# Moving the block sums of the second MLP product into the first, and reordering buffers and the last pair, in an encoder-layer kernel

## The chip, the cores and the metric

The kernel runs on one core of a Trainium2 chip. The metric is the device time of one launch in microseconds (us). The kernel before takes 2404.65 us, the median of three runs (2403.71 to 2405.92).

## The reference

One encoder layer works on two sequences of width 1024: 2048 rows (prompt) and 256 rows (sample), 18 row tiles of 128 in all. Cut to the part that matters here:

```python
def encoder_layer(x, c, ...):
    ...                                   # modulation, mixer: everything before the MLP
    h = modulate(rmsnorm(x, norm_mlp), sh2, sc2)
    x = x + gt2[:, None, :] * (jnp.square(jax.nn.relu(h @ w_mlp_in)) @ w_mlp_out)
    return x
def run_trunk(x, c, ...):
    ...
    return rmsnorm(x, norm_final)
```

`w_mlp_in` is 1024 x 4096 and `w_mlp_out` 4096 x 1024, all in float32.

## The kernel before

Everything up to the mixer's output fills the first 970 us and is untouched. Then come two matrix products, each done as a 2 x 2 block product in seven multiplications instead of eight (`STEPS`, L27: left operand, right operand, accumulator bank X, Y or Z). Four of the seven left operands are sums: S1 to S4, formed from the blocks A11, A12 and A22 and from A21. Each float32 operand is split into a high part (ScalarE cast, L80, `split`) and a low part (VectorE subtraction, L81), and each multiplication is run three times (`three`): high by high, low by high, high by low.

**First product** (L1023 to L1071), about 971 to 1671 us. Three column groups `c` of three row pairs each (a pair is two row tiles), and in each group eight blocks `q` of 512 hidden columns, in the order 0 to 7. The stationary operand is the weight (`wB`, `wT`), the moving one the activation (`opA`, `opS`, 128x384). At the start of groups 1 and 2 VectorE and ScalarE also form the left operands of the group (`form_left`). Each `q` gives two hidden tiles `hid` (ReLU and square on ScalarE, L1055 to L1059), each stored to DRAM in `hidd[c][r]`, where `r = q // 2` is the round of the second product that will read it. For round 3 alone (`j // GJ == NG - 1`, L1062 and L1068) VectorE also forms S2, S3 and S4 in a tile `hs` and S1 in `hid`, and stores seven blocks instead of four (`NB`, L979).

**Second product** (L1152 to L1205). Four rounds `r` over the hidden dimension and, in each, nine pairs `pr`. `load_mo` (L1099) loads the round's weights into raw tiles `t` and `o` (five buffers "raw", two "rawb"), forms sums and splits them into 28 tiles `wo`; there are just 28, so that a weight tile of the next round needs the same tile of the last pair to be done. A pair loads its left blocks into `hr` (pool `hr0` for even `pr`, `hr1` for odd, L1162), forms the four sums on VectorE where only four blocks were stored (L1166 to L1170), splits seven operands into `ho`, multiplies, and adds the banks into `acc` (L1194 on ScalarE in round 0, else L1196 on VectorE). `acc` comes from DRAM and goes back there between rounds. With nine pairs the last pair of a round and the first of the next both use `hr0`. In round 3 `finish_tile` (L1128) multiplies by the gate, adds the residual, normalises and stores; the last pair has its own version, `finish_block` and `finish_rows` (L1138, L1143).

The order of each engine's instructions is set by a scheduler at build time, which also decides where pools let a tile start. Pools lie at addresses in the order in which they are opened (`VB`, L1078), and a pool's tile waits for whatever was at its address before.

Of the kernel before, what the change touches and what calls it, by code (L numbers as in the profile page):

```python
# [31 lines left out]
def encoder(ctx: ExitStack, tc: tile.TileContext, a):  # L32
# [43 lines left out]
    def dram(shape, name):  # L76
        return tc.dram_tile(shape, F32, name=nm(name))
# [901 lines left out]
    NB = [4] * (NG - 1) + [7]  # L979
    hidd = [[dram([NPC, GJ, P, NB[r] * P], "hidd") for r in range(NG)] for _ in range(NC)]  # L980

    def raw_w(s):
        return wt("raw", s, [P, 1024], 8)
# [37 lines left out]
    for c in range(NC):  # L1021
        if c:
            left = left_ops()  # L1023
            for pr in range(NPC):
                hab = []
                for i in range(2):
                    h = raw_w("hr")
                    sp.dma_start(out=h, in_=h2d[2 * (NPC * c + pr) + i])
                    hab.append(h)
                form_left(left, pr, *hab, lambda s: wt("s", s, [P, 512], 4))  # L1030
        for q in range(8):
            w = load_mi(q)
            hid = [wt("hid", "hid", [P, NPC, 4, P], 3) for _ in range(2)]
            at, cp_ = [{}, {}], [{}, {}]
            for i, (ln, rn, bn) in enumerate(STEPS):
                for f in range(2):
                    if i in (0, 1, 3):
                        at[f][bn] = bank(bn)
                    o, kept = at[f][bn], cp_[f]
                    lh, ll = left[ln]  # L1040
                    rh, rl = w[rn]
                    three(lambda p_, k, first, last: add_mm(
                        i, o[:, :CW], (rh, rh, rl)[p_][:, k * 256 + f * P:k * 256 + f * P + P],
                        (lh, ll, lh)[p_][:, k], first, last), range(4))
                    if i in (0, 2, 3):
                        kept[i] = mid("c")
                        act.copy(kept[i], o[:, :CW])
                    hf = hid[f]
                    if i == 1:
                        dve.tensor_tensor(out=hf[:, :, 0, :], in0=cols(o), in1=cols(kept[0]), op=ALU.add)  # L1050
                    elif i == 4:
                        dve.tensor_tensor(out=hf[:, :, 2, :], in0=cols(o), in1=cols(kept[3]), op=ALU.add)
                    elif i == 5:
                        dve.tensor_tensor(out=hf[:, :, 1, :], in0=cols(o), in1=cols(kept[2]), op=ALU.add)
                        act.activation(hf[:, :, 0:3, :], hf[:, :, 0:3, :], AF.Relu)  # L1055
                    elif i == 6:
# [11 lines left out]
                        if j // GJ == NG - 1:  # L1068
# [66 lines left out]
    def halves(b):  # L1135
        return slice(b % 2 * 512, b % 2 * 512 + 512)

    def finish_block(b, y, x1, ss):  # L1138
        dve.tensor_tensor(out=y, in0=y, in1=gate[:, halves(b)], op=ALU.mult)
        dve.tensor_tensor(out=y, in0=y, in1=x1[:, halves(b)], op=ALU.add)  # L1140
        act.activation(x1[:, halves(b)], y, AF.Square, accum_out=ss[:, b % 2:b % 2 + 1])  # L1141

    def finish_rows(t, y, ss):  # L1143
        dve.tensor_tensor(out=ss[:, 2:3], in0=ss[:, 0:1], in1=ss[:, 1:2], op=ALU.add)
        r = rstd_from(ss[:, 2:3], 1, 1.0 / D)
        for b in range(2):
            yb = y[:, 512 * b:512 * b + 512]
            dve.scalar_tensor_tensor(out=yb, in0=yb, scalar=r[:, 0:1], in1=nf[:, halves(b)],
                                     op0=ALU.mult, op1=ALU.mult)
            sp.dma_start(out=xrows("y", t)[:, halves(b)], in_=yb)  # L1150

    for r in range(NG):  # L1152
        w = load_mo(r)
        if r == NG - 1:
            gate = load_gate(1, 0, lambda s: v1(s, "rawb"))
            nf = v1("nf", "rawb")
            sp.dma_start(out=nf, in_=a["norm_final"].rearrange("(o c) -> o c", o=1).to_broadcast([P, D]))
        for pr in range(NT // 2):
            if r == NG - 1 and pr == NP // 2:
                gate = load_gate(1, 1, lambda s: v1(s, "rawb"))  # L1160
            c, pc = divmod(pr, NPC)
            hv = v1("hr", f"hr{pr % 2}").rearrange("p (j b s) -> p j b s", j=GJ, b=7)  # L1162
            sp.dma_start(out=hv[:, :, 0:NB[r], :].rearrange("p j b s -> p j (b s)"),
                         in_=hidd[c][r][pc].rearrange("j p n -> p j n"))
# [6 lines left out]
            acc = v1("acc", "acc").rearrange("p (b n) -> p b n", b=4)  # L1171
            if r:
                sp.dma_start(out=acc, in_=accd[pr].rearrange("p (b n) -> p b n", b=4))
            rows = [acc[:, 2 * i:2 * i + 2, :].rearrange("p b n -> p (b n)") for i in range(2)]
            end = r == NG - 1 and pr == NT // 2 - 1
            if r == NG - 1:
                x1 = [v1("x1", "raw") for _ in range(2)]
                for i in range(2):
                    sp.dma_start(out=x1[i], in_=x1d[2 * pr + i])
            at = {}  # L1180
            ss = [tsm([P, 4], "ss") for _ in range(2)] if end else None
            for i, (ln, rn, bn) in enumerate(STEPS):
# [14 lines left out]
                if end:  # L1197
                    if i not in (0, 2, 3):
                        finish_block(b_, acc[:, b_], x1[b_ // 2], ss[b_ // 2])
                    if i > 4:  # L1200
                        finish_rows(2 * pr + b_ // 2, rows[b_ // 2], ss[b_ // 2])
                elif r == NG - 1 and i > 4:
# [78 lines left out]
```

## Time and profile before

| | |
|---|---|
| profiled execution | 2405.53 us, of which the span is 2403.5 us |
| median of the runs | 2404.65 us |
| TensorE busy | 2326.6 us, 97% of the span |
| VectorE busy | 1539.2 us, 64% |
| ScalarE busy | 1004.5 us, 42% |
| first product | about 971 to 1671 us |
| second product | 1671 us to the end |

A row of the timeline gives start, duration, engine, line, operation, output and input tiles, shapes and count, and in brackets the idle time before it with what ended it. PE is TensorE's multiplication, PEld its weight load, DVE VectorE, ACT ScalarE, POOL GpSimd, SPq the queue that issues transfers. Busy rows overlap a little at their ends, since an instruction's tail runs beside the next one's start.

### The profile page before, as it was taken

How to read it: one execution, taken by the hardware profiler on the slowest of the kernel's cores; microseconds unless marked ns; L12 is line 12 of the kernel's file. 1: busy time of each engine (PE TensorE's matmuls, PEld its weight loads, DVE VectorE, ACT ScalarE, POOL GpSimd, SP SyncE). 2: the span in 40 equal slices, each digit the busy share in tenths (PEclk: the TensorE clock that was granted, in tenths of full speed). 3: DMA queues.
4: the chain of work that ended last, by engine and by line, in shares of the span. 5: the costliest groups of instructions: out<-in, count | busy, mean ns of one | idle time of the engine just before them, and what ended most of it. 6: DMA issues, size and time to landing. Idle time of an engine off the chain costs nothing.

```text
span 2403.5 us, 30791 instructions
## 1 busy us (share of the span) xinstructions
PE 2326.6 (97%) x11905; PEld 2033.9 (85%) x11905; DVE 1539.2 (64%) x2254; ACT 1004.5 (42%) x1686; POOL 115.8 (5%) x191
## 2 busy tenths in 40 slices
PE   7999999999999999999999999999899999999998
PEld 4788887788887888999999999998787788787786
DVE  3676768535444754655785577557756867857788
ACT  4842222223333533555665566556334323224332
POOL 0101100011111000000000000000000000000000
PEclk9999999999999999999999999999999999999999
DMA  8647568433333455543453346433534545546774
GB/s 286 215 144 252 188 217 289 171 99 121 119 103 127 140 171 188 167 131 123 154 184 123 127 156 194 136 120 130 191 105 159 200 158 197 188 158 227 276 255 165
DMA packets 183866, 411.69 MB, mean 171 GB/s; under 512 B 12101, under 2 KB 80485, under 8 KB 176809
## 3 DMA queue, kind: packets, MB, share of 16 engines
q1 hardware_dynamic: 182136, 405.68, 49.2%
q0 software_dynamic: 1584, 4.06, 0.6%
q8 instruction: 93, 1.52, 0.3%
q14 instruction: 53, 0.43, 0.1%
HBM read 274.15 MB, written 135.54 MB: 170 GB/s over the span
## 4 chain that ended last, share of the span: by engine, by line
PE 77%; issue 9%; DVE 6%; DMA 5%; ACT 2%; POOL 1%; SPq 0%; POOLq 0%; DVEq 0%; ACTq 0%
PE mX L963 30%; PE proj L84 18%; PE mZ L963 15%; PE mY L963 7%; PE o L84 2%; DMA ada<-ada_w 1%; PE dft L84 1%; PE tr L745 1%; DMA hr<-hidd 1%; DVE woT L81 1%; PE kvf L84 1%; DVE adacc L356 1%; DVE woB L81 1%; PE sc L84 1%; DVE acc L1196 1%
## 5 line engine op out<-in xcount | busy, mean ns | idle before, releaser
L963 PE MATMUL mX<-woT,ho 128*128 128x512 f32 x1296 | 311.5, 390 | 3.7 <-ACT x L1141 1.5
L80 ACT CAST ho<-hr 128x512 fp32r<-128x512 f32 x252 | 153.1, 621 | 343.3 <-PE mX L963 208.7
L963 PEld LDWEIGHTS mX<-woT,ho 128*128 128x128 f32 x1296 | 242.8, 188 | 56.3 <-issue 1.9
L963 PE MATMUL mX<-opS,wT 128*128 128x384 f32 x1152 | 208.0, 334 | 0.0
L84 PE MATMUL proj<-whi,hhi 128*128 128x512 f32 x720 | 190.1, 402 | 18.3 <-ACT hhi L80 9.4
L963 PEld LDWEIGHTS mX<-opS,wT 128*128 128x128 f32 x1152 | 200.4, 188 | 0.0
L81 DVE TENSOR_TENSOR ho<-hr,ho 128x512 fp32r<-128x512 f32 x252 | 170.4, 687 | 39.7 <-ACT ho L80 39.5
L84 PE MATMUL proj<-wlo,hhi 128*128 128x512 f32 x720 | 185.2, 396 | 0.0
L84 PE MATMUL proj<-whi,hlo 128*128 128x512 f32 x720 | 184.4, 393 | 0.0
L84 PEld LDWEIGHTS proj<-whi,hhi 128*128 128x128 f32 x720 | 132.4, 190 | 47.4 <-ACT hhi L80 10.7
L84 PEld LDWEIGHTS proj<-wlo,hhi 128*128 128x128 f32 x720 | 136.1, 191 | 30.7 <-issue 2.5
L84 PEld LDWEIGHTS proj<-whi,hlo 128*128 128x128 f32 x720 | 133.1, 188 | 30.7 <-issue 4.2
L81 DVE TENSOR_TENSOR wB<-mr,wB 128x1024 fp32r<-128x1024 f32 x72 | 88.0, 1222 | 81.1 <-ACT wB L80 81.0
L1196 DVE TENSOR_TENSOR acc<-mX,acc 128x512 f32<-128x512 f32 x117 | 80.0, 687 | 68.5 <-PE mX L963 55.5
L963 PE MATMUL mY<-woB,ho 128*128 128x512 f32 x432 | 112.2, 396 | 10.0 <-ACT woB L80 6.8
L963 PE MATMUL mX<-woB,ho 128*128 128x512 f32 x432 | 110.8, 396 | 5.6 <-ACT ho L80 5.5
L963 PE MATMUL mZ<-woT,ho 128*128 128x512 f32 x432 | 108.9, 392 | 6.3 <-ACT woT L80 5.5
L105 POOL TENSOR_SCALAR rv<-ss 128x1 f32<-128x1 f32 (+1 forms) x72 | 17.9, 248 | 1885.8 <-ACT x L139 1391.9
L80 ACT CAST wB<-mr 128x1024 fp32r<-128x1024 f32 x72 | 75.4, 1047 | 76.0 <-PE mY L963 41.0
L963 PEld LDWEIGHTS mY<-woB,ho 128*128 128x128 f32 x432 | 81.7, 190 | 30.1 <-ACT woB L80 8.3
L963 PE MATMUL mY<-opA,wB 128*128 128x384 f32 x576 | 104.6, 334 | 2.3 <-DVE x L153 2.3
L963 PE MATMUL mX<-opA,wB 128*128 128x384 f32 x576 | 105.5, 334 | 0.0
(251 smaller groups left out, 4368.9 us busy)
## 6 DMA issues: line engine op xcount, KB each, us to landing
mr<-w_mlp_in SPq DMA_DIRECT2D x96, 512.0 KB
hidd<-hid SPq DMA_DIRECT2D x48, 768.0 KB
hr<-hidd SPq DMA_DIRECT2D x27, 1024.0 KB
accd<-acc SPq DMA_DIRECT2D x27, 1024.0 KB
acc<-accd SPq DMA_DIRECT2D x27, 1024.0 KB
ada<-ada_w SPq DMA_DIRECT2D x48, 512.0 KB
h<-hd SPq DMA_DIRECT2D x36, 512.0 KB
x<-x_prompt SPq DMA_DIRECT2D x32, 512.0 KB
```

The costliest lines, as they stand in the source:

```text
L80: act.copy(hi, src)
L81: dve.tensor_tensor(out=lo, in0=src, in1=hi.bitcast(F32), op=ALU.subtract)
L84: pe.matmul(out, l, r, start=first, stop=last)
L105: pool.tensor_scalar(out=v[:, :n], in0=ss[:, :n], scalar1=scale, scalar2=EPS, op0=ALU.mult, op1=ALU.add)
L356: dve.scalar_tensor_tensor(out=acc_[s_], in0=w, scalar=c2[:, k, s_:s_ + 1], in1=acc_[s_], op0=ALU.mult, op1=ALU.add)
L745: pe.transpose(o[:, hs], src[:, hs], ident)
L963: pe.matmul(out, l, r, start=first and fresh, stop=last, skip_group_check=not fresh)
L1196: dve.tensor_tensor(out=acc[:, b_], in0=o, in1=acc[:, b_], op=ALU.add)
```

## The change

Four things change. (1) `SUMS` lists, for each column group, the rounds whose block sums are formed in the first product: 0, 1 and 3 for groups 0 and 2, 0 and 3 for group 1. The blocks `q` run in the order `QS`, which puts blocks without sums first and last in each group. (2) `hr` and `acc` alternate over all 36 pairs (`side`) instead of within a round. (3) The pools `rawb`, `acc`, `hr1` and `wo3a` swap addresses. (4) The last pair has a function of its own, `last_pair`: products into bank X run as two halves of 256 columns, gate and residual are applied to `acc` ahead of the last products, the sample's gate is loaded at the start of round 3, and the final stores leave from two queues.

```diff
+    SUMS = (0, 1, 3), (0, 3), (0, 1, 3)
+    NB = [[7 if r in SUMS[c] else 4 for r in range(NG)] for c in range(NC)]
+    QS = (4, 0, 1, 2, 3, 6, 7, 5), (2, 4, 0, 1, 6, 7, 3, 5), (4, 6, 7, 0, 1, 2, 3, 5)
...
-        for q in range(8):
+        for q in QS[c]:
...
-                        if j // GJ == NG - 1:
+                        if NB[c][j // GJ] == 7:
...
-    VB = {"wo2b": (1024, 5), "wo2a": (1024, 3), "wo1": (1024, 7), "wo0": (1024, 7), "wo3a": (1024, 2),
-          "hr1": (HB, 1), "acc": (2048, 2), "rawb": (1024, 2), "fill": (512, 1), "raw": (1024, 5),
+    VB = {"wo2b": (1024, 5), "wo2a": (1024, 3), "wo1": (1024, 7), "wo0": (1024, 7), "rawb": (1024, 2),
+          "acc0": (2048, 1), "hr1": (HB, 1), "acc1": (2048, 1), "wo3a": (1024, 2), "fill": (512, 1), "raw": (1024, 5),
...
+    def last_pair(src, acc, x1, rows, w):
...
+        def gate_add(b):
+            y = acc[:, b]
+            dve.tensor_tensor(out=y, in0=y, in1=gate[:, halves(b)], op=ALU.mult)
+            add(y, y, x1[b // 2][:, halves(b)])
...
+        def rows_out(k, rest, early, late):
+            pool.tensor_tensor(out=col(k), in0=col(k), in1=col(rest), op=ALU.add)
+            pool.tensor_tensor(out=col(k), in0=col(k), in1=mhalf[:, 0:1], op=ALU.pow)
+            r = col(k)
+            y = x1[early // 2][:, halves(early)]
+            act.activation(y, y, AF.Copy, scale=r)
+            dve.scalar_tensor_tensor(out=acc[:, late], in0=acc[:, late], scalar=r, in1=nf[:, halves(late)],
                                      op0=ALU.mult, op1=ALU.mult)
+            store(act, early, y)
+            store(sp, late, acc[:, late])
...
+            if i in (0, 1, 3):
+                at[bn] = [(bank("X"), ha), (bank("X"), hb)] if bn == "X" else [(bank(bn), full)]
...
+                if i < 6:
+                    dve.tensor_tensor(out=y, in0=oo, in1=y, op=ALU.add)
+                else:
+                    t = v1("tg", "raw")[:, 0:256]
+                    dve.tensor_tensor(out=t, in0=oo, in1=gate[:, halves(b_)][:, c], op=ALU.mult)
+                    add(y, y, t)
+                    square(b_, 4 + n, c)
...
-            hv = v1("hr", f"hr{pr % 2}").rearrange("p (j b s) -> p j b s", j=GJ, b=7)
+            side = (r * (NT // 2) + pr) % 2
+            hv = v1("hr", f"hr{side}").rearrange("p (j b s) -> p j b s", j=GJ, b=7)
...
-            if NB[r] == 4:
+            if NB[c][r] == 4:
```

VectorE's queue where the second product begins, in the kernel before. `hs` and `hid` belong to the first product's last block, `o` and `t` are raw weights, `wo` their splits, `ho` the split left operands of pair 0.

```order
L236 TENSOR_TENSOR o_14490<-o_14490,t_14487 128x512
L236 TENSOR_TENSOR hs_14310<-hid_14124 128x3x128
L81 TENSOR_TENSOR woT_14430<-t_14487,woT_14430 128x512
L81 TENSOR_TENSOR woB_14421<-o_14467,woB_14421 128x512
L81 TENSOR_TENSOR ho_14590<-hr_14533,ho_14590 128x512
L81 TENSOR_TENSOR ho_14607<-hr_14533,ho_14607 128x512
L81 TENSOR_TENSOR ho_14623<-hr_14533,ho_14623 128x512
L233 TENSOR_TENSOR hid_14124<-hid_14124 128x3x128
L236 TENSOR_TENSOR o_14467<-o_14467,t_14464 128x512
L236 TENSOR_TENSOR hs_14331<-hid_14125 128x3x128
```

The same engine in the changed kernel, from the last instruction on `hid` on.

```order
L1057 TENSOR_TENSOR hid_14257<-mZ_14359,c_14342 128x3x128
L236 TENSOR_TENSOR t_14610<-o_14613,t_14610 128x512
L236 TENSOR_TENSOR o_14611<-o_14613,o_14611 128x512
L81 TENSOR_TENSOR ho_14659<-hr_14656,ho_14659 128x512
L81 TENSOR_TENSOR ho_14676<-hr_14656,ho_14676 128x512
L81 TENSOR_TENSOR ho_14693<-hr_14656,ho_14693 128x512
L236 TENSOR_TENSOR t_14633<-o_14634 128x512
L81 TENSOR_TENSOR woT_14549<-o_14590,woT_14549 128x512
L81 TENSOR_TENSOR woB_14550<-o_14611,woB_14550 128x512
```

From the last `hid` addition to the last split of round 0's weights there were 51 rows (20 `wo`, 14 raw sums, 8 of `hs` and `hid`, 5 `ho`, 3 sums of `hr`, 1 `acc`); now there are 33 (15 `wo`, 10 raw sums, 7 `ho`, 1 `acc`).

SyncE's queue of transfers around the same place, before: `o_14467`, a raw tile of the second of four parts of the weights, is the seventh of the eight that round 0 needs.

```order
L1163 DMA hr_14533<-hidd_8214 128x4x512
L1109 DMA o_14490<-w_mlp_out 128x1024
L1107 DMA o_14511<-w_mlp_out 128x1024
L1109 DMA o_14467<-w_mlp_out 128x1024
L1067 DMA hidd_8225<-hid_14124 128x3x512
L1107 DMA o_15669<-w_mlp_out 128x1024
L1109 DMA o_14513<-w_mlp_out 128x1024
```

And now; its counterpart is `o_14590`, which stands some 55 rows earlier in the queue, among the loads of `w_mlp_in`.

```order
L1236 DMA hr_14656<-hidd_8214 128x4x896
L1112 DMA o_14613<-w_mlp_out 128x1024
L1110 DMA o_14634<-w_mlp_out 128x1024
L1112 DMA o_14636<-w_mlp_out 128x1024
L1110 DMA o_15756<-w_mlp_out 128x1024
L1070 DMA hidd_8224<-hid_14256 128x3x512
```

All of round 0's weights are now asked for ahead of the last stores of `hid`, and the first load of `hr` brings seven blocks instead of four.

VectorE's queue at the very end, before: the last bank read is followed by gate, residual and two scalings.

```order
L1196 TENSOR_TENSOR acc_19384<-mX_19395,acc_19384 128x512
L1139 TENSOR_TENSOR acc_19384<-acc_19384,gate_19380 128x512
L1140 TENSOR_TENSOR acc_19384<-acc_19384,x_19387 128x512
L1144 TENSOR_TENSOR ss_19391<-ss_19391 128x1
L1148 SCALAR_TENSOR_TENSOR acc_19384<-acc_19384,rr_19531,nf_18234 128x512
```

And now: `tg` is the gated half bank; the last two rows belong to two different row tiles.

```order
L1203 TENSOR_TENSOR tg_19646<-mX_19465,gate_18297 128x256
L233 TENSOR_TENSOR acc_19447<-acc_19447,tg_19646 128x256
L1220 TENSOR_SCALAR ss_19454<-ss_19453,ss_19454 128x1
L1179 SCALAR_TENSOR_TENSOR acc_19447<-acc_19447,ss_19453,nf_18299 128x512
L1179 SCALAR_TENSOR_TENSOR acc_19447<-acc_19447,ss_19454,nf_18299 128x512
```

Of the last row tile only one half of the columns is scaled here; the other goes to ScalarE.

## Rows read from the trace of the kernel before

**Rows 1.** Busy time by blocks q of the first product: stretch, length, each engine's busy time
```profile
1380.00:1409.10 29.10, 29.10 (x169) 29.10 (x169) 15.46 (x18) 16.02 (x20) 0.00 (x0) 1.00 0.47 155
1409.10:1438.20 29.10, 29.10 (x170) 29.10 (x169) 26.40 (x43) 20.22 (x33) 0.00 (x0) 1.00 0.52 175
1438.20:1467.40 29.20, 29.20 (x171) 29.20 (x170) 28.41 (x36) 17.79 (x25) 0.00 (x0) 1.00 0.69 218
1467.40:1496.50 29.10, 29.10 (x170) 29.10 (x169) 21.26 (x22) 18.64 (x23) 0.00 (x0) 1.00 0.44 148
1496.50:1525.60 29.10, 29.10 (x170) 29.10 (x168) 16.27 (x17) 15.54 (x20) 0.00 (x0) 1.00 0.40 128
```

**Rows 2.** The same view where rounds begin, and of a stretch inside round 0
```profile
1671.20:1709.40 38.20, 25.46 (x92) 17.86 (x92) 37.17 (x64) 19.70 (x35) 0.00 (x0) 0.82 0.59 209
1760.00:1780.00 20.00, 20.00 (x90) 16.55 (x89) 9.58 (x15) 6.08 (x11) 0.00 (x0) 1.00 0.30 106
1838.00:1884.00 46.00, 41.74 (x176) 32.05 (x176) 43.67 (x74) 25.41 (x47) 0.00 (x0) 1.00 0.62 219
2030.00:2060.00 30.00, 25.68 (x105) 20.14 (x104) 30.00 (x51) 14.97 (x27) 0.00 (x0) 0.94 0.63 235
2205.00:2235.00 30.00, 26.88 (x112) 20.26 (x111) 29.46 (x49) 17.37 (x32) 0.00 (x0) 1.00 0.81 293
```

**Rows 3.** Timeline where the second product begins
```profile
1659.43 0.39 SPq L1163 DMA_DIRECT2D hr<-hidd  x1
...
1666.15 1.14 ACT L80 CAST ho<-hr 128x512 fp32r<-128x512 f32 x2 [3.15 <-DMA hr<-hidd]
...
1669.68 0.55 DVE L1054 TENSOR_TENSOR hid<-mZ,c 128x384 f32<-128x384 f32 x1
...
1681.56 1.22 PE L963 MATMUL mZ<-woT,ho 128*128 128x512 f32 x2 [5.03 <-ACT woT L80]
...
1688.79 2.07 PE L963 MATMUL mY<-woB,ho 128*128 128x512 f32 x4 [6.01 <-ACT woB L80]
...
1694.93 3.02 PE L963 MATMUL mX<-woT,ho 128*128 128x512 f32 x12 [0.16 <-ACT acc L1194]
...
1699.19 0.68 DVE L81 TENSOR_TENSOR woT<-o,woT 128x512 fp32r<-128x512 f32 x1
1699.79 0.68 DVE L236 TENSOR_TENSOR hr<-hr 128x512 f32<-128x512 f32 x1
```

**Rows 4.** Waits of SyncE's queue, 1640 to 1706 us: who, for whom, total, times, longest
```profile
SPq L1109 <- DVE hid L1054: 8.5, 1, 8.5
```

**Rows 5.** Waits of TensorE between rounds 1 and 2 and between rounds 2 and 3
```profile
PE mX L963 <- ACT ho L80: 2.7, 1, 2.7
PE mY L963 <- DVE woB L81: 1.7, 1, 1.7
...
PE mY L963 <- DVE woB L81: 1.4, 1, 1.4
PE mX L963 <- ACT ho L80: 0.9, 1, 0.9
```

**Rows 6.** Groups of VectorE instructions in the first product: busy us, mean ns, idle before
```profile
L236 DVE TENSOR_TENSOR hs<-hid 128x384 f32<-128x384 f32 x20 | 11.1, 554 | 6.7 <-ACT hid L1059 6.7
```

**Rows 7.** Timeline of 256-column matmuls in an early stage
```profile
245.54 0.28 PE L84 MATMUL pb<-yl,mh 128*128 128x256 f32 x1
245.66 0.28 PE L84 MATMUL pb<-yh,ml 128*128 128x256 f32 x1
...
245.54 0.19 PEld L84 LDWEIGHTS pb<-yh,ml 128*128 128x128 f32 x1
```

**Rows 8.** Timeline of the end
```profile
2391.51 3.00 PE L963 MATMUL mX<-woT,ho 128*128 128x512 f32 x12 [1.49 <-ACT x L1141]
...
2394.86 0.68 DVE L1196 TENSOR_TENSOR acc<-mX,acc 128x512 f32<-128x512 f32 x1
2395.58 0.69 DVE L1139 TENSOR_TENSOR acc<-acc,gate 128x512 f32<-128x512 f32 x1
2396.30 0.69 DVE L1140 TENSOR_TENSOR acc<-acc,x 128x512 f32<-128x512 f32 x1
2397.03 0.63 ACT L1141 ACTIVATE x<-acc 128x512 f32<-128x512 f32 x1 [3.41 <-DVE acc L1140]
...
2398.89 1.41 DVE L1148 SCALAR_TENSOR_TENSOR acc<-acc,rr,nf 128x512 f32<-128x512 f32 x2 [0.94 <-POOL rr L108]
```

**Rows 9.** Transfers from 2385 us to the end: GB/s in 40 slices
```profile
GB/s 89 18 0 0 0 0 0 0 0 89 399 416 230 0 0 0 0 0 0 0 0 31 368 390 341 4 0 0 0 0 0 0 0 168 390 390 186 0 0 0
```

More of the change, by code (lines that the diff above doesn't have):

```diff
@@ L977, in encoder @@
     w_mo = a["w_mlp_out"][0].rearrange("(f p) n -> p f n", p=P)
-    NB = [4] * (NG - 1) + [7]
-    hidd = [[dram([NPC, GJ, P, NB[r] * P], "hidd") for r in range(NG)] for _ in range(NC)]
+    SUMS = (0, 1, 3), (0, 3), (0, 1, 3)
+    NB = [[7 if r in SUMS[c] else 4 for r in range(NG)] for c in range(NC)]
+    hidd = [[dram([NPC, GJ, P, NB[c][r] * P], "hidd") for r in range(NG)] for c in range(NC)]
+    QS = (4, 0, 1, 2, 3, 6, 7, 5), (2, 4, 0, 1, 6, 7, 3, 5), (4, 6, 7, 0, 1, 2, 3, 5)
     def raw_w(s):
@@ L1136, in halves, with col, left_op, square @@
         return slice(b % 2 * 512, b % 2 * 512 + 512)
[L1138 to L1148, printed above, removed]
-                                     op0=ALU.mult, op1=ALU.mult)
-            sp.dma_start(out=xrows("y", t)[:, halves(b)], in_=yb)
+    def last_pair(src, acc, x1, rows, w):
+        full, ha, hb = slice(0, 512), slice(0, 256), slice(256, 512)
+        s_lo, s_hi = tsm([P, 4], "ss"), tsm([P, 4], "ss")
+        ho = {}
+        junk = v1("tj", "raw")
+        def col(k):
+            return (s_lo, s_hi)[k // 4][:, k % 4:k % 4 + 1]
+        def left_op(i):
+            t = v1("ho", f"ho{nho[0] // 3 % 2}", F32R)
+            nho[0] += 1
+            ho[i] = t[:, 0:512], t[:, 512:1024]
+            split(src[STEPS[i][0]], *(x.rearrange("p (j s) -> p j s", j=GJ) for x in ho[i]))
+        def gate_add(b):
+            y = acc[:, b]
+            dve.tensor_tensor(out=y, in0=y, in1=gate[:, halves(b)], op=ALU.mult)
+            add(y, y, x1[b // 2][:, halves(b)])
+        def square(b, k, c=full):
+            act.activation(junk[:, c], acc[:, b][:, c], AF.Square, scale=1.0 / 32,
+                           accum_out=col(k))
+        def gain(b):
+            dve.tensor_tensor(out=x1[b // 2][:, halves(b)], in0=acc[:, b], in1=nf[:, halves(b)], op=ALU.mult)
+        def store(eng, b, y):
+            eng.dma_start(out=xrows("y", NT - 2 + b // 2)[:, halves(b)], in_=y)
+        def rows_out(k, rest, early, late):
[5 more added lines that the diff above has]
+            dve.scalar_tensor_tensor(out=acc[:, late], in0=acc[:, late], scalar=r, in1=nf[:, halves(late)],
+                                     op0=ALU.mult, op1=ALU.mult)
+            store(act, early, y)
+            store(sp, late, acc[:, late])
+        left_op(0)
+        gate_add(2)
+        at = {}
+        for i, (ln, rn, bn) in enumerate(STEPS):
+            if i < 6:
+                left_op(i + 1)
+            if i in (0, 1, 3):
+                at[bn] = [(bank("X"), ha), (bank("X"), hb)] if bn == "X" else [(bank(bn), full)]
+            hh, hl = ho[i]
+            b_ = ADDR[i]
+            for n, (o, c) in enumerate(at[bn]):
+                oo = o[:, 0:c.stop - c.start]
+                three(lambda p_, j, first, last: add_mm(
+                    i, oo, (hh, hh, hl)[p_][:, j * P:(j + 1) * P], w[j][rn][p_ % 2][:, c], first, last), range(GJ))
+                y = acc[:, b_][:, c]
+                if i < 6:
+                    dve.tensor_tensor(out=y, in0=oo, in1=y, op=ALU.add)
[4 more added lines that the diff above has]
+                    square(b_, 4 + n, c)
+            if i == 1:
+                gate_add(0)
+                square(0, 0)
+                gain(0)
+                dve.tensor_scalar(out=col(6), in0=col(0), scalar1=EPS, scalar2=None, op0=ALU.add)
+            elif i == 4:
+                gate_add(3)
+                square(3, 3)
+                gain(3)
+            elif i == 5:
+                gate_add(1)
+                square(1, 1)
+                rows_out(1, 6, 0, 1)
+            elif i == 6:
+                dve.tensor_scalar(out=col(7), in0=col(3), scalar1=col(4), scalar2=EPS,
+                                  op0=ALU.add, op1=ALU.add)
+                rows_out(5, 7, 3, 2)
@@ L1154, in encoder @@
         if r == NG - 1:
-            gate = load_gate(1, 0, lambda s: v1(s, "rawb"))
+            gate, gate_s = (load_gate(1, i, lambda s: v1(s, ("rawb", "raw")[i])) for i in range(2))
             nf = v1("nf", "rawb")
@@ L1179, in encoder @@
                     sp.dma_start(out=x1[i], in_=x1d[2 * pr + i])
+            if end:
+                last_pair(src, acc, x1, rows, w)
+                break
             at = {}
-            ss = [tsm([P, 4], "ss") for _ in range(2)] if end else None
             for i, (ln, rn, bn) in enumerate(STEPS):
@@ L1196, in encoder @@
                     dve.tensor_tensor(out=acc[:, b_], in0=o, in1=acc[:, b_], op=ALU.add)
[L1197 to L1202, printed above, removed]
+                if r == NG - 1 and i > 4:
                     finish_tile(2 * pr + b_ // 2, rows[b_ // 2], x1[b_ // 2])
```

8 lines of the change are left out of this document (4 added, 4 removed).

## The prediction

> **What bounds the kernel now.** I read the page's busy shares first: TensorE has 97% of the span, so a gain must come from places where it stands idle, and the question is where these are. A view of busy time by blocks shows it. Through the first product TensorE is busy without a gap, in every block of 29.1 us [rows 1]. Inside a round of the second product it is also full: 20.00 of 20.00 us, with VectorE at 9.6 [rows 2]. There twelve 512-column matmuls follow in 2.72 us, 0.227 us each. The idle time sits where rounds begin, and there VectorE is the full one: 37.2 of 38.2, 43.7 of 46, 30.0 of 30 and 29.5 of 30 us [rows 2]. By the counts of matmuls in these four rows (92, 176, 105, 112) at 0.227 us, TensorE lost about 17.4, 6.1, 6.2 and 4.6 us, 34 in all. It waits there for weight tiles and for split left operands, from ScalarE and VectorE [rows 3, 5]. The rest is the end: a wait of 1.49 us ahead of the last product and about 9 us from its end to the end of the span [rows 8]. So some 43 us lie open, and most of that is VectorE's queue at five places.
>
> **First product, what is added.** Five more pairs of group and round get sums, two blocks q each: 10 blocks with 8 VectorE instructions of 128x384. One takes 0.554 us [rows 6], so 4.4 us a block, 44 us in all. A block without other work has VectorE busy 16.3 us of 29.1 [rows 1]; it becomes 20.7. The dangerous blocks are those where a group begins: VectorE is at 28.4 of 29.2, after 26.4 of 29.1 in the block ahead [rows 1]. The new order of q puts blocks without sums there, so the 26.4 falls by 4.4 and the 28.4 stays; in group 2 the next one (21.3) gets 4.4 more, 25.7. The 20 extra stores of 576 KB fall in blocks with the transfer engines at 0.40 [rows 1]. Cost taken: nothing, hidden beside TensorE's own work. The bounds are 0 and 44 us (all on the path); I take the lower since the blocks of round 3 already do this (26.4 us of VectorE in 29.1) and TensorE shows 29.10 of 29.10 [rows 1].
>
> **Where the second product begins.** In the trace the last addition into hid starts on VectorE at 1669.68 and the last split of round 0's weights at 1699.19, one instruction per 0.6 us [rows 3]. That run had 51 instructions, now 33: the 8 of the last block's sums and the 3 of hr are gone, 9 of the weights' now stand ahead of it, and 2 more splits of ho behind. The reason is a queue: a raw load (L1109) waited 8.5 us for VectorE's additions into hid [rows 4], since its pool lay where the first product's tiles were; with that pool elsewhere the load stands some 55 places earlier. The product that TensorE started at 1694.93 needs the fourth part of one weight; its split is now the 24th instruction after the last hid addition, so done at about 1670.2 + 24 x 0.6 = 1684.6, and the product's first matmuls can run a little ahead of that. TensorE has 31 matmuls (7.0 us) to do first, so it is there at 1678.3 and loses 5 to 6 us where it lost 17. What is late next: the last split (33rd, 1690.0) comes before its product, and hr for pair 1, now 1.8 MB instead of 1.0, behind two hid stores. A 1 MB load took 1659.43 to 1666.15 [rows 3] in company; 0.8 MB more is about 2 us at the 400 GB/s that the busiest slices reach [rows 9]. I add 2 us for it. Lost then: 7.5 instead of 17.4, gain 10. Bounds: all 17.4 back, or only the 8 removed hid and hs instructions with no use of the earlier loads (8 x 0.47 = 4, since 0.55 us instructions follow at about 0.47).
>
> **Where rounds 1, 2 and 3 begin.** The load of hr for the first pair no longer waits for the last pair's buffer. Round 0 to 1: between the last pair's first split and the second pair's last, VectorE has 79 instructions instead of 89 (10 sums gone, 6 us), and lost time was 6.1. The weight tiles (28 splits and 16 raw sums, 26 us) remain and can't start before the last pair gives its tiles back, so not all returns: gain 3.5, between 0 and 6.1. Round 1 to 2: 96 instructions as before, as round 2 has no prepared sums. The wait of 2.7 us on a split left operand [rows 5] should shrink, the 1.7 on a weight stay: gain 2, between 0 and 4.5. Round 2 to 3: 81 as before; of 0.9 us on a left operand and 1.4 on a weight [rows 5] I take back 1, between -1 and 3. Inside rounds the dropped sums are worth nothing, since VectorE has half its time free there [rows 2]; larger loads of hr in 15 pairs (0.75 MB each) go beside transfer engines at 0.30.
>
> **The end.** Halving the products into bank X makes 96 matmuls of 256 columns out of 48 of 512. In an early stage such matmuls, each with a fresh weight load, start 0.12 us apart [rows 7], so 96 x 0.12 - 48 x 0.227 = +0.6 us. The Trainium skill speaks against halving: "TensorE: Matmul & The Clock Gate", section "The mechanism", has a weight load overlap matmuls in flight only where it goes to other row groups, so that each load would stand in the path. The trace disagrees, with loads of 0.19 us beside matmuls 0.12 us apart [rows 7]; what the rule would make of the time is rival (e). After the last matmul there were add, gate and residual at about 0.7 us each, a square, a reciprocal root, and two scalings in a row [rows 8]. Now: a gate and an add of 256 columns. No row has these on VectorE; 128x384 took 0.55 and 128x512 0.68, so about 0.41 by the same slope (bounds 0.16, a 128x1 instruction, and 0.55). That is 0.85 instead of 2.15, 1.3 less. The half square saves 0.2, the second scaling 0.66 (it runs on ScalarE), together 2.2. The wait of 1.49 ahead of the last product came from VectorE being behind with reading bank X. Its queue is as full now (33 instructions from the reading of the second-last pair's third product on, where 26 stood), but two half banks let TensorE go on with one while VectorE reads the other. I take 0.5, between nothing and the whole 1.49. So the last matmul ends 0.5 us earlier (1.0 less wait, 0.6 more matmul time). Against it: both last stores now become ready at once, and they share the same engines: 512 KB at 390 GB/s [rows 9] are 1.3 us wherever they are issued, so the 0.66 of the second scaling was cover and gives nothing. Gain 2.0, between -1 and 4. The sample's gate is loaded at the start of round 3 instead of ahead of its use; that is inside this count.
>
> **Sum.** 10 + 3.5 + 2 + 1 + 2 = 18.5 us off the profiled execution (2405.53: span 2403.5 and 2.0 around it), so 2387.0 there. The median of the runs lies 0.9 below the profiled one, which I carry over: 2386.1.
>
> **Rivals.**
> (a) *The beginning of the second product stays as slow, bound by transfers.* Eight raw tiles of 512 KB and 1.8 MB of hr are 6 MB, 15 us at 400 GB/s, much of it after the last buffers come free; the 6.01 us wait for woB stood behind such a load [rows 3]. For it: the larger hr stands ahead of three raw loads. Against it: those three waited for buffers that now come free sooner. Gain 3 instead of 10: 2393.
> (b) *The change doesn't do there what it says.* At the second and third change of rounds VectorE has as many instructions as before, and it was full [rows 2]; the wait for left operands then turns into one for weights. The three gains fall from 6.5 to 1: 2391.6.
> (c) *The first product becomes the place.* VectorE takes its instructions in order; a sum waits for ScalarE's square (6.7 us of such waits in round 3's blocks [rows 6]), and the next block's weight splits queue behind it. It decides once VectorE is later than the second buffer of weights, one block. Then each of the 10 blocks loses its 4.4 us: 2386 + 44 = 2430, slower. Against it: no such loss in round 3's blocks [rows 1].
> (d) *More comes back than I count*: the beginning loses 3 and each change of rounds 2: 14 + 11 + 2 = 27, 2377.
> (e) *Weight loads show between the half products.* At 0.19 + 0.12 us for each of 96 matmuls [rows 7] the end costs 29.8 instead of 10.9 us, 18.9 more less the 0.6 counted: 2404, no change. This is the time by the rule cited above; the trace's 0.12 us speaks against it.
>
> **How the numbers follow.** Forecast 0.58 (2380 to 2390.5), (a) 0.13, (b) 0.12, (d) 0.08, (c) 0.05, (e) 0.02, and 0.02 for small mishaps that leave no gain. Measurements of this kernel can't tell 0.2%, 4.8 us, from no change, so faster means under 2399.8: forecast, (a), (b) and (d), 0.91. Within 0.2%: (e) and the mishaps, 0.04. Slower: 0.05 from (c). The range takes in forecast, (a) and (b), 0.83: 2379 to 2395.
>
> **What would show it.** Right: TensorE without a gap in all 24 blocks; about 7 to 8 us lost in the first 38 us of the second product, no raw load waiting for hid, VectorE's full run there some 10 us shorter; about 3, 4 and 4 us lost at the changes of rounds; half products 0.12 us apart and the last one followed by some 7 us instead of 9. Wrong: any wait of TensorE between 1000 and 1670 us, a wait of ScalarE's casts on hr or raw weights at 1670 to 1690, or half products further apart than 0.12 us.

## The result and the profile after

The changed kernel takes 2386.76 us (median of four runs, 2386.16 to 2394.11), the kernel before 2404.24 in the same comparison: ratio 0.9929 [0.9917, 0.9941], 17.5 us faster. The forecast was 2386.1. The profiled execution took 2386.19, its span 2384.2, which is 19.3 less than the span before.

To find where the 19.3 us came from, I measured one thing in all traces: where the starts of two matmuls of the second product that follow each other lie more than 0.227 us apart, the excess is lost time. Summed by place (us):

| place | before | after | gain | predicted |
|---|---|---|---|---|
| beginning of the second product | 17.7 | 4.9 | 12.9 | 10 |
| round 0 to 1 | 6.6 | 2.8 | 3.8 | 3.5 |
| round 1 to 2 | 6.7 | 6.4 | 0.3 | 2 |
| round 2 to 3 | 5.0 | 4.9 | 0.1 | 1 |
| last pairs: waits | 2.1 | 0.9 | 1.2 | 1.0 |
| last pairs: 96 half products for 48 whole ones | | | -0.6 | -0.6 |
| last matmul's start to the end of the span | 9.4 | 8.4 | 0.9 | 1.5 |
| start of the second product | 1671.2 | 1670.1 | 1.1 | 0 |

The gains make 19.7, 0.4 more than the 19.3; what loses the 0.4 is in no row. The last row is nothing of the change. That start lies between 1669.8 and 1676.3 us in the kernels below, whatever was changed, and almost all of it is set where the first product begins (967.5 us before, 966.4 after): from the first matmul of the first product to the first of the second it is 703.7 us in both.

Busy time of the kernel after in the stretches of [rows 2], shifted with the work: where the second product begins, inside round 0, and at the three changes of rounds; the last two rows are blocks of the first product, as in [rows 1]. Columns: stretch, length, busy time of PE, PEld, DVE, ACT, POOL, then the granted clock, the transfers' share, GB/s.

```profile
1670.20:1708.40 38.20, 35.22 (x149) 27.16 (x148) 28.19 (x47) 22.45 (x40) 0.00 (x0) 1.00 0.74 269
1750.00:1770.00 20.00, 20.00 (x90) 16.57 (x89) 6.79 (x11) 6.20 (x12) 0.00 (x0) 1.00 0.40 145
1820.00:1866.00 46.00, 44.63 (x192) 35.31 (x191) 40.95 (x67) 26.51 (x49) 0.00 (x0) 1.00 0.72 273
2012.00:2042.00 30.00, 26.71 (x106) 20.17 (x105) 30.00 (x51) 14.09 (x25) 0.00 (x0) 0.94 0.71 259
2187.00:2217.00 30.00, 26.75 (x113) 20.39 (x112) 29.01 (x48) 16.96 (x31) 0.00 (x0) 1.00 0.92 350
1029.60:1058.70 29.10, 29.10 (x170) 29.10 (x169) 20.18 (x25) 15.54 (x20) 0.00 (x0) 1.00 0.50 168
1175.20:1204.30 29.10, 29.10 (x170) 29.10 (x169) 26.57 (x43) 20.31 (x33) 0.00 (x0) 1.00 0.51 174
```

At the beginning there are 149 matmuls where 92 stood, and VectorE is busy for 28.2 us where it was for 37.2. At the change to round 1 VectorE is no longer full; at the changes to rounds 2 and 3 it still is (30.00 and 29.01 of 30). The first product has no gap, with sums (20.18 us of VectorE, predicted 20.7) or at a group's end (26.57).

The waits of TensorE at that beginning (1669 to 1709 us; columns: who, for whom, total, times, longest). The 5.0 and 6.0 us of [rows 3] are gone:

```profile
PE mZ L963 <- ACT woT L80: 1.4, 1, 1.4
PE mZ L963 <- ACT ho L80: 0.8, 1, 0.8
PE mX L963 <- ACT woB L80: 0.3, 1, 0.3
PE mX L963 <- ACT acc L1269: 0.3, 1, 0.3
```

The wait of 8.5 us of a raw load for an addition into `hid` [rows 4] is gone; one such wait is left in SyncE's queue, 1640 to 1706 us:

```profile
SPq L1110 <- DVE hid L1053: 1.9, 1, 1.9
```

A part of the gain is clock. In the kernel before, behind a wait of 5.0 us, TensorE was granted the lower of its two levels (1.2 of 2.4 GHz) for ten microseconds, in which it ran six matmuls; in the profiled execution after the change the clock is 1.00 there. Windows 1681 to 1691 us, before and then after:

```profile
1681.00:1691.00 10.00, 3.29 (x6) 1.66 (x6) 10.00 (x19) 3.20 (x6) 0.00 (x0) 0.50 0.87 294
```
```profile
1681.00:1691.00 10.00, 9.69 (x43) 7.70 (x42) 8.10 (x14) 3.52 (x7) 0.00 (x0) 1.00 0.75 257
```

Waits make 12.7 us of the 17.7 before and 2.8 of the 4.9 after; the rest is matmuls spaced wider than 0.227 us around them, at the lower clock among others.

The 4.9 has some luck in it. Two kernels below (e9_lastq, e11_addr_q) have the same waits there, 2.9 and 2.7 us, but in their profiled executions the granted clock fell behind them, and the twelve matmuls that follow the last wait took 4.60 us instead of 3.02. First the kernel after, then e11_addr_q:

```profile
1681.83 3.02 PE L963 MATMUL mX<-woT,ho 128*128 128x512 f32 x12 [0.31 <-ACT acc L1269]
```
```profile
1681.65 4.60 PE L963 MATMUL mX<-woT,ho 128*128 128x512 f32 x12 [0.34 <-ACT acc L1269]
```

In e6_full, with waits of 3.0 us, it did not fall. So about 1.6 us of the 12.9 depend on which level TensorE had in that execution.

The end, as a timeline of the kernel after (answers to [rows 8]; start, duration, and in brackets the idle time before and its end):

```profile
2369.60 3.03 PE L963 MATMUL mX<-woT,ho 128*128 128x256 f32 x24
...
2372.96 3.10 PE L963 MATMUL mX<-woT,ho 128*128 128x256 f32 x24 [0.32 <-DVE acc L1200]
...
2376.53 0.42 DVE L1203 TENSOR_TENSOR tg<-mX,gate 128x256 f32<-128x256 f32 x1
2376.99 0.43 DVE L233 TENSOR_TENSOR acc<-acc,tg 128x256 f32<-128x256 f32 x1
...
2379.64 0.75 DVE L1179 SCALAR_TENSOR_TENSOR acc<-acc,ss,nf 128x512 f32<-128x512 f32 x1 [0.71 <-POOL ss L1175]
2380.40 0.37 ACTq L1171 DMA_DIRECT2D y_sample<-x  x1
```

The half products start 0.120 us apart and cost 0.6 us, as worked out; the wait of 1.49 us ahead of the last product is 0.32; a 256-column gate or addition takes 0.42 us (estimate 0.41).

### The profile page after: what moved, and what is told of

Its sections match the earlier page's. It is cut to its first block, busy times and chain, and to the rows that moved or that the text cites. A ratio compares the mean times of both kernels' runs of the same rounds, so it can differ in the third digit from the quotient of the medians.

```text
span 2384.2 us, 30997 instructions
## 1 busy us (share of the span) xinstructions
PE 2323.0 (97%) x11953; PEld 2033.5 (85%) x11953; DVE 1542.1 (65%) x2280; ACT 1005.9 (42%) x1690; POOL 115.2 (5%) x191
## 5 line engine op out<-in xcount | busy, mean ns | idle before, releaser
L963 PE MATMUL mX<-woT,ho 128*128 128x512 f32 (+1 forms) x1332 | 311.4, 384 | 0.8 <-DVE acc L1200 0.3
L963 PE MATMUL mX<-woB,ho 128*128 128x512 f32 (+1 forms) x444 | 111.0, 389 | 3.6 <-ACT ho L80 1.5
L963 PE MATMUL mZ<-opS,wT 128*128 128x384 f32 x576 | 104.3, 334 | 0.0
```

What stands on the lines that cost most here:

```text
L963: pe.matmul(out, l, r, start=first and fresh, stop=last, skip_group_check=not fresh)
```

## The experiments

All runs were timed beside the kernel before (2405.92, 2404.92 and 2405.10 us in the three series). The row of the kernel after has its time from the result above. The table gives time, ratio with its interval, and lost time by place in the profiled execution; the text below refers to it. The places depend on the execution too: the change from round 0 to 1 lost 6.6 and 5.5 us in two kernels that are alike there (before and e4_last), so differences of about 1 us are not sure.

| kernel | us | ratio | begin | 0-1 | 1-2 | 2-3 | last pairs |
|---|---|---|---|---|---|---|---|
| before | | | 17.7 | 6.6 | 6.7 | 5.0 | 2.1 |
| after | 2386.76 | 0.9929 [0.9917, 0.9941] | 4.9 | 2.8 | 6.4 | 4.9 | 0.9 |
| e1_side | 2403.07 | 0.9987 [0.9978, 0.9996] | 18.0 | 4.2 | 6.2 | 4.9 | 2.2 |
| e2_place | 2415.63 | 1.0038 [1.0024, 1.0051] | 28.3 | 6.2 | 6.4 | 5.0 | 2.0 |
| e3_sums | 2397.92 | 0.9967 [0.9954, 0.9979] | 12.0 | 2.9 | 6.4 | 5.6 | 1.8 |
| e4_last | 2405.42 | 0.9997 [0.9988, 1.0005] | 18.3 | 5.5 | 6.8 | 5.0 | 0.9 |
| e5_order | 2409.11 | 1.0016 [1.0007, 1.0025] | 26.1 | 3.0 | 6.4 | 5.7 | 0.9 |
| e6_full | 2391.23 | 0.9940 [0.9928, 0.9952] | 5.0 | 3.0 | 6.4 | 5.6 | 1.8 |
| e7_all | 2411.06 | 1.0026 [1.0016, 1.0035] | 25.8 | 2.9 | 5.8 | 6.9 | 0.9 |
| e8_c0 | 2390.79 | 0.9940 [0.9927, 0.9953] | 6.3 | 3.1 | 5.4 | 4.9 | 1.2 |
| e9_lastq | 2388.99 | 0.9935 [0.9921, 0.9948] | 6.6 | 2.7 | 6.4 | 5.0 | 0.9 |
| e10_addr | 2406.18 | 1.0005 [0.9996, 1.0014] | 21.1 | 2.9 | 6.2 | 4.8 | 0.9 |
| e11_addr_q | 2389.49 | 0.9933 [0.9920, 0.9945] | 6.4 | 3.1 | 6.4 | 4.9 | 0.9 |
| e12_pool | 2412.01 | 1.0029 [1.0018, 1.0039] | 18.6 | 4.3 | 8.8 | 9.1 | 0.4 |

**One part alone, on the kernel before.** The first, the alternation of `hr` and `acc`:

```diff
+            side = (r * (NT // 2) + pr) % 2
-            hv = v1("hr", f"hr{pr % 2}")...
+            hv = v1("hr", f"hr{side}")...
+            acc = v1("acc", f"acc{side}")...
```

For that the pool `acc` of two tiles becomes two pools of one, `acc0` and `acc1`, at the same place.

> The kernel before with one edit: hr and acc alternate over all 36 pairs. Theory Q (VectorE's queue sets the lost time where rounds begin): hardly any gain, 0 to 2 us, lost time at the three changes of rounds stays within 1 us of 6.6, 6.7 and 4.9. Rival B (the buffer that the last pair and the next first pair share sets it): each of the three loses some 2 us less, 5 to 7 us in all, about 2398.

Measured: 2403.07. It acts at one place, the change from round 0 to 1: 6.6 to 4.2.

The second, the new addresses:

```diff
-    ... "wo3a": (1024, 2), "hr1": (HB, 1), "acc": (2048, 2), "rawb": (1024, 2), ...
+    ... "rawb": (1024, 2), "acc0": (2048, 1), "hr1": (HB, 1), "acc1": (2048, 1), "wo3a": (1024, 2), ...
```

> The kernel before with the pools rawb, acc, hr1 and wo3a at the changed kernel's addresses, nothing else. Theory Q (the last block's sums and hr's sums in VectorE's queue set the 17.7 us lost where the second product begins): a gain of at most 4 us, 13 to 17 us still lost there. Rival P (the raw load that waits 8.5 us for the first product's tiles sets it): 8 to 12 us come back from the placement alone, about 2394.

Measured: 2415.63, slower than before by some 10 us. The prediction's reason, the raw load that waits for `hid`, is mended in this kernel, and yet the beginning loses 28.3 us. Its waits of TensorE (1640 to 1710 us) and of ScalarE (1666 to 1712) say why:

```profile
PE mX L963 <- ACT acc L1194: 15.1, 1, 15.1
```
```profile
ACT acc L1194 <- DMA hidd<-hs: 12.4, 1, 12.4
```

The first accumulator now lies where `hs` was. In the plain order of q the last block belongs to round 3, so it has sums, and `hs` is stored last of all. ScalarE's first copy out of a bank X must wait for that store, and TensorE for the bank.

The third, the sums and the order of q, on the addresses of before:

```diff
+    SUMS = (0, 1, 3), (0, 3), (0, 1, 3)
+    QS = (4, 0, 1, 2, 3, 6, 7, 5), (2, 4, 0, 1, 6, 7, 3, 5), (4, 6, 7, 0, 1, 2, 3, 5)
-        for q in range(8):
+        for q in QS[c]:
```

> The kernel before with the prepared sums and the order of q, old placement, old buffers, old last pair. Theory Q: the beginning loses 6 to 9 us less, the change from round 0 to 1 loses 3 to 4 less, the other two stay; 2392 to 2395. Rival P: the raw load still waits for the first product's tiles, so the beginning loses at most 3 us less; 2398 or more. Rival C (sums in the first product cost): TensorE idle between 1000 and 1670 us.

Measured: 2397.92, although its second product began 5 us later than in the kernel before. The beginning loses 12.0: a last block without sums shortens VectorE's queue, but a raw load still waits for `hid` (SyncE's queue, 1646 to 1706 us), and TensorE has waits of 4.0 us for a weight and 2.8 for the first accumulator:

```profile
SPq L1112 <- DVE hid L1057: 5.7, 1, 5.7
```
```profile
PE mZ L963 <- ACT woT L80: 4.0, 1, 4.0
PE mX L963 <- ACT acc L1197: 2.8, 1, 2.8
```

The fourth, the last pair's function:

```diff
-            ss = [tsm([P, 4], "ss") for _ in range(2)] if end else None
+            if end:
+                last_pair(src, acc, x1, rows, w)
+                break
```

> The kernel before with the new last pair alone. From the traces of before and after the end is worth 1.2 us less waiting in round 3 (2.1 to 0.9) and 1.1 us less from the last matmul on, with 0.6 us more matmul time: 1.5 to 3 us, about 2402, the rest of the kernel as before. Rival: the end gained only because the rest shifted, then 0 to 1 us.

Measured: 2405.42, no difference that its interval shows. The trace has 1.2 us less waiting and 0.9 less after the last matmul (8.5 for 9.4) against 0.6 for the halves: 1.5 us, too small to be seen in the time.

At the beginning the parts do not add up: sides -0.3 us, addresses -10.6, sums and order +5.7, last pair -0.6, and all together +12.9. Addresses and order act on each other.

**One part undone, on the kernel after.** Plain order of q:

```diff
-        for q in QS[c]:
+        for q in range(8):
```

> The changed kernel with the blocks q in plain order 0 to 7, so that blocks with sums stand at both ends of each group and of the first product. Theory Q: the second product's beginning gets its 8 hs and hid instructions back (8 x 0.47 = 4 us of VectorE), 3 to 6 us more lost there, about 2391; TensorE stays without a gap at the groups' beginnings, as it did before with 26 of 29 us. Rival C: VectorE at 28 to 29 of 29 us where a group begins makes TensorE wait, 4 us or more at each of two groups, 2395 or more.

Measured: 2409.11; the whole gain is gone and more. TensorE waits for nothing in the first product (1000 to 1668 us), so this is not the order within groups. The beginning loses 26.1, and ScalarE shows the wait of the second run (1666 to 1712 us):

```profile
ACT acc L1269 <- DMA hidd<-hs: 18.5, 1, 18.5
```

The last pair's halves taken out:

```diff
-                at[bn] = [(bank("X"), ha), (bank("X"), hb)] if bn == "X" else [(bank(bn), full)]
+                at[bn] = [(bank(bn), full)]
```

> The changed kernel with the last pair's products into bank X in one piece of 512 columns. The halves cost 0.6 us of matmul time and save an add and gate of 256 columns each and a wait after the last matmul; by VectorE's durations (0.68 against 0.42) two instructions and half a square, 0.5 + 0.2 us, and a wait of about 1 us for the bank ahead of the last product. Theory: 0.5 to 1.5 us slower. Rival: same within 0.3 us, because VectorE's queue sets the end either way.

Measured: 2391.23, 4.5 us more than the kernel after, but its interval overlaps, and in its profiled execution 3.5 us of that are a later start of the second product. The wait ahead of the last product comes back (timeline of its end):

```profile
2377.70 2.97 PE L963 MATMUL mX<-woT,ho 128*128 128x512 f32 x12 [1.22 <-DVE acc L1200]
...
2380.71 0.69 DVE L1203 TENSOR_TENSOR tg<-mX,gate 128x512 f32<-128x512 f32 x1 [0.23 <-PE mX L963]
```

So of the 1.2 us less waiting in the last pairs, 0.9 are the halves' (1.8 against 0.9), and from the last matmul's start to the end the halves save 0.4 (8.9 against 8.4).

Sums in all rounds and groups, and in round 2 of group 0 only:

```diff
-    SUMS = (0, 1, 3), (0, 3), (0, 1, 3)
+    SUMS = ((0, 1, 2, 3),) * 3             # e7_all
+    SUMS = (0, 1, 2, 3), (0, 3), (0, 1, 3) # e8_c0
```

> The changed kernel with sums prepared for all groups and rounds, so that no pair forms them. Theory Q: the changes from round 1 to 2 (6.4 us lost) and 2 to 3 (4.9) fall to what round 0 to 1 has now, about 3, since 11 of 96 instructions leave VectorE's queue at the first; at the second its count near the change stays at 81, so less there, 0 to 2. The second product's beginning gets 4 us of hs work back. In all between 3 us faster and 3 slower, 2384 to 2390. Rival B (transfers and buffers, not VectorE's count): the changes of rounds stay at 6.4 and 4.9.

> The changed kernel with round 2's sums prepared in group 0 too, that is for the first three pairs of round 2, which stand right behind the change from round 1 to 2. Theory Q: that change loses 3 to 4 us less (11 of 96 instructions go), the rest stays, 2383 to 2384. Rival B: it stays at 6.4 us. Rival C: group 1's first block, with the last block of group 0 now at 26 of 29 us of VectorE's time ahead of it, makes TensorE wait.

Measured: 2411.06 and 2390.79. With sums in all rounds the last block (q = 5) has them too, and the wait for the store of `hs` is back (18.9 us on ScalarE, 25.8 lost). At the change from round 1 to 2 theory Q expected about 3 us lost instead of 6.4, and 5.8 are lost; at 2 to 3 it is 6.9 instead of 4.9. Without the 12 left sums of group 0 in round 2 alone (e8_c0) the change to that round loses 5.4 instead of 6.4, where theory Q expected 3 to 4 us less; VectorE is still full there (30.00 of 30 us), now with weights, and TensorE's longest wait is for a cast that itself waited for a raw weight. Waits of TensorE and of ScalarE in that kernel (2014 to 2050 us):

```profile
PE mY L963 <- ACT woB L80: 1.7, 1, 1.7
```
```profile
ACT woB L80 <- DMA o<-w_mlp_out: 4.1, 1, 4.1
```

**What the order has to do.** Three kernels more, on that of after. In the first only the last two blocks of the last group are exchanged, all else in plain order; the second has the plain order everywhere and another tile where `hs` was; the third has these addresses and the order of the kernel after.

```diff
-    QS = (4, 0, 1, 2, 3, 6, 7, 5), (2, 4, 0, 1, 6, 7, 3, 5), (4, 6, 7, 0, 1, 2, 3, 5)
+    QS = (0, 1, 2, 3, 4, 5, 6, 7), (0, 1, 2, 3, 4, 5, 6, 7), (0, 1, 2, 3, 4, 6, 7, 5)  # e9_lastq
...
-          "acc0": (2048, 1), "hr1": (HB, 1), "acc1": (2048, 1), "wo3a": (1024, 2), "fill": (512, 1), ...
+          "wo3a": (1024, 2), "fill": (512, 1), "hr1": (HB, 1), "acc1": (2048, 1), "acc0": (2048, 1), ...  # e10_addr, e11_addr_q
```

> The kernel after, with blocks q in plain order in groups 0 and 1; only in group 2 does 5 stay behind 7. Theory H (the first accumulator lies where hs was, so ScalarE's first copy out of bank X waits for the last store of hs; only the very last block matters): entry loses about 5 us as in the kernel after, 2387 us, ratio 0.993. Rival P (the new order pays inside the first product, at the beginnings of groups): gaps of TensorE at 1200 or 1437 us, and some of the 22 us that the plain order cost come back, 2395 to 2409.

Measured: 2388.99, with 6.6 us lost at the beginning, of which 1.6 are the clock shown above. One exchange does all that the order does, as far as the runs can tell. Groups 1 and 2 now begin with sums, and VectorE is full for whole blocks there; TensorE has no gap all the same (busy time of two blocks of this kernel):

```profile
1204.00:1233.00 29.00, 29.00 (x170) 29.00 (x169) 29.00 (x38) 20.10 (x29) 0.00 (x0) 1.00 0.63 201
1440.00:1469.00 29.00, 29.00 (x169) 29.00 (x168) 29.00 (x37) 19.07 (x26) 0.00 (x0) 1.00 0.71 223
```

> The kernel after with plain order of q in all groups, but with wo3a (round 3's weights) and fill at the address of hs, and acc0 behind acc1. Theory H: the wait of 18.5 us of ScalarE's copy for the store of hs goes, entry loses 6 to 10 us instead of 26 (the last block's sums still stand in VectorE's queue), 2387 to 2392 us. Rival Q (the wait is only where VectorE's longer queue shows; the sums of the last block are what costs): entry stays above 18 us, 2400 or more.

Measured: 2406.18; 21.1 us lost, a miss of theory H in the form given. The accumulator no longer waits, but `wo3a` serves the fourth part of round 0's weights too, which I had overlooked, and now ScalarE's cast into it waits for `hs` (timeline):

```profile
1687.72 1.42 SPq L1074 DMA_DIRECT2D hidd<-hs  x2
...
1693.31 0.62 ACT L80 CAST woB<-o 128x512 fp32r<-128x512 f32 x1 [6.86 <-DMA hidd<-hs]
...
1693.98 2.08 PE L963 MATMUL mX<-woB,ho 128*128 128x512 f32 x4 [3.12 <-ACT woB L80]
```

The store leaves at 1687.7 and has landed at 1693.3. Of the 21 us lost 4.1 are a wait for a split `ho` ahead of that; this split is no later than in the kernel after, but TensorE has 6 matmuls to do before it where it had 19. What the sums in VectorE's queue cost by themselves this run does not show.

> The kernel after, with the same addresses as in the run before this one and its own order of q. Theory H: nothing waits for hs any more in the kernel after (0.3 us on the first accumulator), so no difference, 2386 to 2388 us; a loss of 2 us or more would mean that the first accumulator at its new place waits for the last additions into hid.

Measured: 2389.49; the intervals overlap. 6.4 us are lost at the beginning against 4.9, with the same waits (2.7 us and 2.8); the difference is the clock shown above. With a last block without sums it makes no difference which of these two lies at the place of `hs`.

**What is left at the changes of rounds.** Two of the four raw sums of each weight block on GpSimd:

```diff
-            sub(b[:, hi], b2[:, hi], b[:, hi])
+            pool.tensor_tensor(out=b[:, hi], in0=b2[:, hi], in1=b[:, hi], op=ALU.subtract)
...
-                    sub(src[n], src["B21"], src["T2"])
+                    pool.tensor_tensor(out=src[n], in0=src["B21"], in1=src["T2"], op=ALU.subtract)
```

> The kernel after, with two of the four raw sums of each weight block (T3 and T4) on GpSimd: 8 fewer VectorE instructions, 4.8 us of its queue, where each round begins; a GpSimd addition of this size takes 1.3 us. Theory V (what is left at the changes of rounds is VectorE's queue): lost at 1 to 2 and 2 to 3 falls from 6.4 and 4.9 us to about 4 and 3, in all some 5 us less, 2382 us. Rival C (the chain from freed weight tile to raw load, sum, cast and split is the bound, whatever the queue): nothing there or 1 us more each, 2387 to 2392 us.

Measured: 2412.01, which neither theory had: the changes to rounds 2 and 3 lose 8.8 and 9.1 us instead of 6.4 and 4.9, and the beginning, which the expectation left out, 18.6 instead of 4.9. Two things go wrong. The first, where round 2 begins:

```profile
2030.41 1.61 POOL L1121 TENSOR_TENSOR o<-o,t 128x512 f32<-128x512 f32 x1 [11.42 <-DVE woB L81]
2030.78 1.78 DVE L81 TENSOR_TENSOR woB<-o,woB 128x512 fp32r<-128x512 f32 x1
```

This VectorE instruction, which meets one of GpSimd, takes 1.78 us instead of 0.68: it ends half a microsecond after GpSimd's. The Trainium skill names such a conflict: "SBUF — State Buffer", section "Who interferes with whom", has a VectorE instruction with two inputs in SBUF (the memory on the chip that both work from) contend with one of GpSimd that reads SBUF. The trace agrees, with 1.78 against 0.68 us. Summed over the nine moved sums from 2010 to 2068 us, such longer instructions put 6.1 us into VectorE's queue, and the sums, at 0.6 us each, take 5.4 out of it; for the seven from 2190 to 2240 us it is 4.0 and 4.2. So the queue hardly became longer.

The second is the moved sums themselves. Some of them take far longer than VectorE's 0.68 us while VectorE goes on beside them, up to 7.2 us at the beginning, and what stands behind them in ScalarE's queue comes late with them. Where round 3 begins:

```profile
2227.63 4.63 POOL L1116 TENSOR_TENSOR o<-o,o 128x512 f32<-128x512 f32 x1 [9.10 <-DVE t L236]
...
2232.30 0.62 ACT L80 CAST woT<-o 128x512 fp32r<-128x512 f32 x1 [2.74 <-POOL o L1116]
...
2234.01 2.95 PE L963 MATMUL mX<-woB,ho 128*128 128x512 f32 x8 [1.96 <-ACT ho L80]
```

So the run does not tell the two theories apart: it lengthened the chain from raw load to split weight and did not shorten VectorE's queue.

## Why the prediction was right

**First product: nothing.** Right: the added sums made 20.2 us of a block, 20.7 expected. At the groups' ends VectorE's 26.4 us fell to 22.6 at one and stayed at 26.6 at the other, where I had let both fall. There was more room than argued: e9_lastq shows VectorE full for whole blocks without a gap of TensorE. Rival (c) fails by that.

**Beginning of the second product: 10 predicted, 12.9 measured.** Right in size, and both parts of the reason are real: sums and order give 5.7 with the addresses of before, and the rest of the change another 7 on top (the addresses, since sides and last pair alone do nothing there). But one step was left out. The prediction followed what the address of `rawb` does and never asked what comes to lie where `hs` was. That is the first accumulator, and alone the new addresses cost 10.6 us. The change works since the last block has no sums, which I had counted as 8 VectorE instructions (4 us); it is worth 21 us in the kernel after (26.1 against 4.9). The lower bound I gave, "only the 8 removed hid and hs instructions", was too high for the mechanism at stake. Rival (a), bound by transfers, fails: hr for pair 1 arrives late (ScalarE waits 5.9 us for it), but TensorE does not wait there, so the 2 us that I added for it were not lost. Most of the surplus over 10 is this; with the lower clock of e11_addr_q 1.6 us of it would be gone. The count of VectorE's queue held. The 24th instruction behind the last `hid` addition is the split that I named, and it was done 24 x 0.6 us behind that addition; I had 1684.6 us because I took the addition 1.7 us later than it came (VectorE in the kernel after; the first of the two `woT` is the 24th):

```profile
1667.99 0.55 DVE L1057 TENSOR_TENSOR hid<-mZ,c 128x384 f32<-128x384 f32 x1
...
1682.30 1.29 DVE L81 TENSOR_TENSOR woT<-t,woT 128x512 fp32r<-128x512 f32 x2
```

**Round 0 to 1: 3.5 predicted, 3.8 measured.** The alternating sides alone give 2.4, the sums alone 3.7, both 3.8: either shortens what the other would, so the terms do not add.

**Rounds 1 to 2 and 2 to 3: 3 predicted, 0.4 measured.** Here rival (b) was right. The failed step is "should shrink, the 1.7 on a weight stay: gain 2". At 1 to 2 the wait on left operands did shrink and the one on a weight stayed, but the gain did not come: the waits fell from 4.3 to 3.2 us in all, and wider spacing around them grew from 2.4 to 3.2. At 2 to 3 the waits are as long as before, 3.1 and 3.2 us, and now all on weights, as rival (b) has it (waits of TensorE in the kernel after, to be held against [rows 5]; 1 to 2 first, then 2 to 3):

```profile
PE mY L963 <- DVE woB L81: 1.9, 1, 1.9
PE mX L963 <- ACT ho L80: 0.7, 1, 0.7
PE mX L963 <- DVE ho L81: 0.5, 1, 0.5
```
```profile
PE mZ L963 <- ACT woT L80: 1.6, 1, 1.6
PE mZ L963 <- DVE woT L81: 1.0, 1, 1.0
PE mX L963 <- ACT woB L80: 0.6, 1, 0.6
```

VectorE was full and stayed so, with the same number of instructions there. The idle time also lowers the granted clock, here to 0.87 over ten microseconds:

```profile
2020.00:2030.00 10.00, 8.06 (x30) 6.20 (x29) 10.00 (x18) 3.95 (x7) 0.00 (x0) 0.87 0.49 164
```

That VectorE's queue is the bound there, as the first paragraph of the prediction has it, is not shown. Twelve instructions less, 7.2 us at 0.6 us each, give only 1.0 us back (e8_c0); no sums at all in round 2 give 0.6 at one change and nothing at the other (e7_all); and what comes last in e8_c0 is a raw weight. That speaks for a large part of the chain from a freed weight tile to its raw load, sums and split; how much of the 6.4 is its part stays open.

**The end: 2.0 predicted, 1.5 measured.** Of the wait 1.2 us came back (1.0 counted), 0.9 of it by the halves, which cost 0.6 as counted; after the last matmul 0.9 came back of 1.5. Rival (e) fails: weight loads did not stretch the half products, which start 0.120 us apart. So the rule of the Trainium skill that the prediction cites ("TensorE: Matmul & The Clock Gate", section "The mechanism") does not hold for this stream of loads. The same section also lets a load run ahead that goes to a background weight buffer, which the prediction left out; where these loads go no run shows. On its own this part is below what the runs can tell.

In sum an error of +2.9 at the beginning, one of -2.6 at two changes of rounds, -0.5 at the end and 1.1 us of another start made a forecast that is closer than its steps. That it came within 1 us is luck; that it came within a few is not, since the largest term was right in its mechanism.

## What to carry to other kernels

When pools are given new addresses, list for each new tenant what lay there before and which instruction frees it last; a gain at one address can be a larger loss at its neighbour. Where one phase hands over to the next, the last block's tail (here an extra tile and its store) is in the path, so put the block with the least behind it last. An engine that is busy all through a change of phase need not be what bounds it: here fewer instructions gave little back, and the same work on GpSimd cost more than it saved.

## What was not expected

- VectorE and GpSimd: a VectorE addition or subtraction of 128x512 that met one of GpSimd took up to 1.78 us, 0.68 alone; the GpSimd ones took 2.31 and 1.51 us on average (one line each), the longest 7.2.
- TensorE's clock takes part in such waits: granted 0.50 for ten microseconds behind the waits of the kernel before, 0.67 on average over 40 us in the run with the new addresses alone, 1.00 in the kernel after, and 0.83 over ten microseconds in e11_addr_q with the same waits as there.
- Ahead of the first product all these kernels are alike, and yet it begins anywhere from 965.5 to 972.6 us, more than a third of the gain apart; single spans have to be compared from the second product on.
